# Which operand tiles of three Strassen stages start at a shifted SBUF address

## The chip, the cores and the metric

The kernel runs on one core of one Trainium2 chip. The metric is the device time of one execution in microseconds (us); lower is better. Before the change it is 2397.99 us, the median of three runs (2395.8 to 2398.48).

## The reference

One layer of a hybrid decoder over 16 meta tokens and 512 real tokens, width 2048, all in float32:

```python
u = rmsnorm(h, norm1_g[l])
proj = u @ w_in[l]                       # 2048 -> 10240
v_pool, v_lru, v_gelu, g_pool, g_lru = jnp.split(proj, IN_SPLITS, axis=-1)
pool_out = pool_mixer(v_pool, pool_w[l], pool_scale[l])
xc = causal_depthwise_conv(v_lru, conv_w[l], conv_b[l])
lru_out = rg_lru(xc, ...) * jax.nn.gelu(v_gelu)
merged = jax.nn.sigmoid(g_pool) * pool_out + jax.nn.sigmoid(g_lru) * lru_out
h = h + merged @ w_out[l]
u2 = rmsnorm(h, norm2_g[l])
h = h + jnp.square(jax.nn.relu(u2 @ mlp_w1[l])) @ mlp_w2[l]   # 2048 -> 8192 -> 2048
...
return rmsnorm(h, final_g)[:, N_META:]
```

## The kernel before

Every product is made from float32 split in two parts, `hi` (rounded) and `lo` (the rest), and three matmuls: weight hi by data hi, weight hi by data lo, weight lo by data hi. The helper `mm3` (its matmul is L365 of the profile) issues these three for one tile of 128 rows; the weights are the stationary operand, the data (128 x 256) the moving one. So the moving operand's start addresses follow the pattern hi, lo, hi for each tile.

The program has these stages, in this order: input projections with the recurrence and the pooling (PSUM tiles `ps_v`, `ps_vl`, `ps_vp`, `ga`, `ps_pw`), the *gates* (`ps_Agl`, `ps_Bge`, ... one pass of `strassen` for each of three segments and eight channel blocks, 24 passes), the output projection (`ps_wo`, 512 columns, no Strassen), *MLP 1* (`ps_A`, `ps_B`, `ps_C`, 32 passes), *MLP 2* (`ps_Ab`, `ps_Bb`, `ps_Cb`: two passes of `strassen_pair`, which take two t at a time, 27 of `strassen` for t = 5 to 31, then three pairs and a single one), and the last norm (`ps_w2l`, `ps_n`).

One pass of `strassen` is seven products in the order x11 (into A), t1 (B), t2 (A), x21 (C), t3 (A), x22 (B), t4 (A). In the gates and MLP 1 each product has eight tiles of data, that is 24 matmuls, and a pass has 168. The data of these seven operands stay in SBUF for the whole stage, in two large tiles `a1` and `a2`, at addresses that `place` gives and `fill` loads. Weights stream in through SP's queue (L104), and ACT (L134) and DVE (L135, L125) split and add them.

In MLP 2 the data are the *slots*: slot j is made by pass j of MLP 1, is stored to DRAM and loaded again into one of nine places (`places`, place j % 9) by POOL's queue (`load_slot`, L1023), 896 KB at a time, and is split into hi and lo by ACT (L1035) and DVE (L1036) in `split_slot`. Pass t (t = 8 to 31) uses the eight slots t-8 to t-1, one tile of each in every product; slot t is split in the middle of pass t and slot t+1 is loaded behind it.

Almost all data tiles start at the same address modulo 256 bytes. A few don't:

- gates: the eight tiles of x22 lie 264 elements apart and not 256, so tile k starts 32 k bytes further on, modulo 256;
- MLP 1: the same for t2;
- MLP 2: in six of the nine places the hi part of x11 alone is moved by 64 or 160 bytes (`gaps`, in elements); the lo part, and all other operands, are not.

What is set by address and what by order: PE's instructions stand in the order in which the program issues them; a scheduler places the work of the other engines, and each DMA queue is served in order.

Of the kernel before, what the change touches and what calls it, by code (L numbers as in the profile page):

```python
# [11 lines left out]
F32 = mybir.dt.float32  # L12
F32R = mybir.dt.float32r
# [4 lines left out]
P = 128  # L18
# [4 lines left out]
TH = T // 2  # L23
HS = SEQ // 2
# [7 lines left out]
B0 = META + HS  # L32
JS = 31
WIN = 8

ORDER = [(JS + q) % 8 for q in range(8)]

# [128 lines left out]
def build(ctx, tc, nc, xt_d, par_d, w_in_d, gate_d, pool_d, woa_d, wob_d, woc_d, w1_d, w2_d, w2t_d,  # L166
          out_d):
    V, S, G, PE = nc.vector, nc.scalar, nc.gpsimd, nc.tensor
# [31 lines left out]
    PL = 16 * TH  # L200
    a1_pool = ctx.enter_context(tc.tile_pool(name="a1", bufs=1))
    a1 = a1_pool.tile([P, 4 * PL + 6 * HS], F32R, name="a1")
# [1 line left out]
    ht = x_stage.enter_context(tc.tile_pool(name="xp", bufs=1)).tile([P, KD, T], F32, name="ht")  # L204
    a2 = None

    def place(i, width=HS):

        if width > HS:
            return [tuple(a1[:, i * PL + (8 * j + k) * width : i * PL + (8 * j + k) * width + HS]  # L210
                          for j in range(2)) for k in range(8)]
        if i < 6:
            t, at = (a1, i * PL) if i < 4 else (a2, (i - 4) * 16 * HS)
            return [tuple(t[:, at + (8 * j + k) * HS : at + (8 * j + k + 1) * HS] for j in range(2))
                    for k in range(8)]
        u = [a1[:, 4 * PL + u * HS : 4 * PL + (u + 1) * HS] for u in range(6)]
        u += [a2[:, 32 * HS + u * HS : 32 * HS + (u + 1) * HS] for u in range(10)]
        return [(u[k], u[8 + k]) for k in range(8)]

    def fill(i, src, n, width=HS):  # L220

        if width > HS:
            t = a1[:, i * PL : i * PL + 16 * width].rearrange("p (a k n) -> p a k n", a=2, k=8)
            src = src.rearrange("p a (k n) -> p a k n", k=8)
            for j in range(2):
                G.dma_start(t[:, j, n, :HS], src[:, j, n].bitcast(F32R))
        elif i < 6:
            t, at = (a1, i * PL) if i < 4 else (a2, (i - 4) * 16 * HS)
            n = slice(n.start * HS, n.stop * HS)
            t = t[:, at : at + 16 * HS].rearrange("p (a n) -> p a n", a=2)[:, :, n]  # L230
            G.dma_start(t, src[:, :, n].bitcast(F32R))
        else:
            flat = src.rearrange("p a n -> p (a n)").bitcast(F32R)
            G.dma_start(a1[:, 4 * PL :], flat[:, : 6 * HS])
            G.dma_start(a2[:, 32 * HS :], flat[:, 6 * HS :])
# [60 lines left out]
    def slots_of(t):  # L296
        return range(max(0, t - WIN), min(t, JS))

    for g in groups:
        def part(n, h):  # L300
            xs = [w2_d[t % WIN + 8 * n, h, :, slots_of(t)[0] * P : (slots_of(t)[-1] + 1) * P] for t in g]
            return xs if len(xs) > 1 else xs[0]
# [45 lines left out]
    y_sp = [dram.tile([P, (7 if j < JS else 4) * HS], F32, name=f"ysp{j}") for j in range(32)]  # L348
# [3 lines left out]
    f_sp = {r: dram.tile([P, 2, 8 * HS], F32, name=f"fsp_{r}") for r in ("x11", "t2", "x21", "t3", "x22", "t4")}  # L352
    g_sp = {r: dram.tile([P, 2, 8 * HS], F32, name=f"gsp_{r}") for r in ("t2", "t3", "x22", "t4")}
# [14 lines left out]
    with ExitStack() as mx:  # L368
# [68 lines left out]
        xc, xs, pend = {}, {}, []  # L437
# [184 lines left out]
        for kind, i in jobs:  # L622
            table[kind](i)
            if (kind, i) == ("VP", 15):
                for q, r in ((0, "x11"), (1, "t2"), (2, "x21"), (6, "t3")):
                    fill(q, f_sp[r], slice(0, 8))
                fill(3, f_sp["x22"], slice(0, 8), TH)
            elif (kind, i) == ("GA", 7):
                W.free["w21"] = 2
        fill(5, f_sp["t4"], slice(0, 8))  # L630
# [136 lines left out]
    def put_plain(e, by_half=False):  # L767
# [12 lines left out]

    X = {r: place(i, TH if r == "x22" else HS) for r, i in (
        ("x11", 0), ("t2", 1), ("x21", 2), ("x22", 3), ("t1", 4), ("t4", 5), ("t3", 6))}
    with tc.tile_pool(name="gp", bufs=1, side="right", reuse_waits="tile") as gp:
        for c in range(8):
# [30 lines left out]
    for i in range(8):  # L817
        G.dma_start(merged(i), m_sp[i].bitcast(F32R).rearrange("p (a s) -> p a s", a=4))

    X = {r: place(i, TH if r == "t2" else HS) for r, i in (  # L820
        ("t2", 0), ("t3", 1), ("x22", 2), ("t4", 3), ("x11", 4), ("t1", 5), ("x21", 6))}
    wo_stage = ExitStack()
    wo = wo_stage.enter_context(tc.tile_pool(name="wo", bufs=1, side="right", reuse_waits="tile"))
# [49 lines left out]
    def forms(p, h, u):  # L873
# [5 lines left out]
        t1, t2 = t[:, :HS], t[:, HS:]  # L879
        put_hl(x11, *X["x11"][p])  # L880
        put_hl(x21, *X["x21"][p])
# [24 lines left out]
    for ch in range(KD):  # L906
        hi, lo = W.next()
# [10 lines left out]
    def refill(q):  # L918

        r = ("t2", "t3", "x22", "t4")[q]  # L920
        fill(q, g_sp[r], slice(0, 6), TH if q == 0 else HS)
        if r in held:
            for i, x in enumerate(X[r][6]):
                G.dma_start(x, held[r][:, i * HS : (i + 1) * HS])
# [15 lines left out]
    for p in range(3, 6):  # L940
        h = None if p == 3 else load_x(p)
        ts3 = []
        for a in range(2):
            t = bank("wo", f"{p}_{a}", SEQ)
# [3 lines left out]
            if (p, a) == (3, 0):  # L948
# [4 lines left out]
                h = load_x(3)  # L953
# [5 lines left out]
    for i in range(2):  # L959
# [4 lines left out]
        for q in (2 * i, 2 * i + 1):  # L964
            hi, lo = W.next()
# [38 lines left out]
    def at(r, n=1):  # L1004
        i = SLOT.index(r)
        return slice(i * HS, (i + n) * HS)

    def shift(pool, name, n=8):

        V.memset(pool.tile([P, n], F32, name=name), 0.0)  # L1010

    slots, early, n = {}, late.enter_context(ExitStack()), 14 * HS
    gaps = {1: 16, 2: 40, 3: 16, 7: 40, 8: 16, 0: 40}
    places = {i: a[:, q * step : q * step + n + gaps.get(i, 0)]
              for a, held, step in ((a1, (1, 2, 3, 7, 8), n + 64), (a2, (4, 5, 6), n)) for q, i in enumerate(held)}

    def load_slot(j, queue):  # L1020
        if j < JS:
            s = slots[j] = places[j % (WIN + 1)]
            queue.dma_start(s[:, : 7 * HS].bitcast(F32), y_sp[j])  # L1023

    def slot(j, r):

        s, a = slots[j], slice(0, 6 * HS) if r is None else at(r)
        h = 13 * HS + gaps.get(j % (WIN + 1), 0) if r == "x11" else 7 * HS + a.start
        return s[:, h : h + a.stop - a.start], s[:, a]

    def split_slot(j):
# [12 lines left out]
    for j in range(32):  # L1044
        if j:
            y = yp.tile([P, 4 * HS], F32, tag="y", name=f"y{j}")
        if j == 1:
            s0 = early.enter_context(tc.tile_pool(name="s0", bufs=1, side="right", reuse_waits="tile"))
            places[0] = s0.tile([P, 14 * HS + 40], F32R, name="slot0")
            shift(s0, "shift0", 32)  # L1050

        def of(r, n=1):
            c = at(r, n)
            return y[:, c.start - 4 * HS : c.stop - 4 * HS]

        def put(c, x, z):
            o = of("x" + c)
            if z is not None:
                V.tensor_tensor(o, x, z, op=ALU.add)
            if c == "12":  # L1060
                o = of("x11", 2)
                V.scalar_tensor_tensor(o, o, 0.0, rho, op0=ALU.max, op1=ALU.mult)
            elif c[0] == "2":
                n = int(c[1]) - 1
                V.scalar_tensor_tensor(o, o if n else x, 0.0, rho[:, n * HS : (n + 1) * HS],
                                       op0=ALU.min, op1=ALU.mult)

        if j == 4:
            load_slot(0, nc.gpsimd)
        strassen(j, X.get, put, **{0: dict(head=head, middle=middle), 8: dict(between=lambda: split_slot(0)), 31: dict(hooks=last)}.get(j, {}))  # L1070
        S.activation(y, y, AF.Square)
        if j >= JS:
            if j < 31:
                nc.gpsimd.dma_start(y_sp[j], y)
            continue
        nc.gpsimd.dma_start(y_sp[j][:, 4 * HS :], y[:, : 3 * HS])
        x21, x22, x11, x12 = (of(r) for r in ("x21", "x22", "x11", "x12"))
        tt = yp.tile([P, 4 * HS], F32, tag="t", name=f"t{j}")
        t1, t2, t3, t4 = (tt[:, at(r)] for r in ("t1", "t2", "t3", "t4"))
        V.tensor_tensor(t1, x11, x12, op=ALU.subtract)  # L1080
        V.tensor_tensor(t3, x22, x12, op=ALU.subtract)
        V.scalar_tensor_tensor(t2, x22, -1.0, t1, op0=ALU.mult, op1=ALU.subtract)
        V.scalar_tensor_tensor(t4, t2, -1.0, x21, op0=ALU.mult, op1=ALU.subtract)
        nc.gpsimd.dma_start(y_sp[j][:, : 4 * HS], tt)
# [11 lines left out]
    for n, g in enumerate(groups):  # L1096
        t = g[0]
# [7 lines left out]
        if t < JS + 2:  # L1105
            for x, e in zip(g, es):
                nc.gpsimd.dma_start(h_sp[x % WIN], e, accum_op=ALU.add)
        if n < 4:
            load_slot(n + 5, nc.gpsimd)
        elif t >= WIN:  # L1110
            load_slot(t + 1, nc.gpsimd)
# [29 lines left out]
    n = 64 - 2 * JS  # L1141
# [35 lines left out]
    for i in range(2):  # L1177
        sums, alone = [], []
        for m in range(KD):
            if i == 0 and m % 4 == 0:  # L1180
                parts.append(W.next())
            hi, lo = parts[m // 4]
            t = ps.tile([P, 512], F32, tag="ps", name=f"ps_w2l_{i}_{m}")[:, :HS]
            c = slice(i * HS, (i + 1) * HS)
            for k in range(n):
                s = slice((m % 4) * n * P + k * P, (m % 4) * n * P + (k + 1) * P)
# [3 lines left out]
            h = ht[:, m // 2, i, m % 2]  # L1190
            V.tensor_tensor(h, t, h, op=ALU.add)  # L1191
            whole = m < 2
            q = hp.tile([P, HS], F32, tag=f"ss{m}" if whole else "ft", name=f"sqo{i}_{m}", bufs=2 if whole else 6)
# [11 lines left out]
            if i == 1 and m == 5:  # L1205
                r = root(0, pend)
# [5 lines left out]
    r = root(1, total(1, pend))  # L1212
# [50 lines left out]
```

## Time and profile before

| what | value |
|---|---|
| median of three runs | 2397.99 us |
| time of the profiled execution | 2397.97 us |
| its span, first to last instruction | 2396.2 us |
| PE busy | 2355.8 us (98%), 19254 matmuls |
| DVE, ACT, POOL busy | 1921.9 (80%), 1212.7 (51%), 313.1 us (13%) |
| TensorE clock granted, mean | 0.995 |

The profiled execution lies 0.02 us from the median, and 1.8 us of it is outside the span. PE is busy nearly all the time, but a busy PE is not yet a PE at its peak: records of matmuls overlap, and how far apart their starts lie says what one costs.

### The profile page before, as it was taken

To read this page: it belongs to the slowest core of one execution; us is meant where nothing else is said; L and a number is where in the kernel's file an instruction comes from. 1 tells how busy PE (TensorE), PEld (TensorE's weight loads), DVE (VectorE), ACT (ScalarE), POOL (GpSimd) and SP (SyncE) were. 2 spreads that over 40 slices of the span, in tenths; PEclk is the share of its full clock that TensorE was granted. 3 is DMA by queue.
4 is the path that set the end of the run, shared out by engine and by line. 5 is a ranking of instruction groups with operands and counts; after the bars stand their busy time and mean duration, and the time that the engine had idled before them with its cause. 6 is when DMAs were issued, how large, how long until landed. Compare 5 with 4: busy or idle time off the path is not lost. (4 is left out here: it accounts for less than half of the span.)

```text
span 2396.2 us, 46247 instructions
## 1 busy us (share of the span) xinstructions
PE 2355.8 (98%) x19254; PEld 2307.7 (96%) x19254; DVE 1921.9 (80%) x2357; ACT 1212.7 (51%) x1632; POOL 313.1 (13%) x429
## 2 busy tenths in 40 slices
PE   8999999999999999999999999999989999999997
PEld 8999999999999999887999999999989999999997
DVE  7867766588888887378989888888879888888877
ACT  6654645355555554244444444444455555555545
POOL 0224342300000001033000000000010000000013
PEclk9999999999999999999999999999999999999999
DMA  5255555754444447568544444555576666666663
GB/s 198 89 167 170 174 176 165 255 190 147 142 149 142 149 152 260 181 202 285 179 161 152 156 157 154 164 165 162 168 226 173 182 178 184 192 187 182 180 184 111
DMA packets 118354, 418.73 MB, mean 175 GB/s; under 512 B 14016, under 2 KB 21312, under 8 KB 116480
## 3 DMA queue, kind: packets, MB, share of 16 engines
q1 hardware_dynamic: 77040, 253.40, 33.0%
q0 software_dynamic: 40960, 162.29, 21.1%
q8 instruction: 150, 2.46, 0.4%
q14 instruction: 60, 0.49, 0.1%
q10 hardware_dynamic: 144, 0.10, 0.0%
HBM read 324.89 MB, written 90.31 MB: 173 GB/s over the span
## 5 line engine op out<-in xcount | busy, mean ns | idle before, releaser
L135 DVE TENSOR_TENSOR wlo<-raw,whi 128x1024 fp32r<-128x1024 f32 (+2 forms) x388 | 466.7, 1205 | 123.5 <-ACT whi L134 122.6
L134 ACT ACTIVATE whi<-raw 128x1024 fp32r<-128x1024 f32 (+2 forms) x388 | 399.0, 1034 | 323.3 <-issue 81.4
L134 ACT ACTIVATE whi<-sum 128x1024 fp32r<-128x1024 f32 (+3 forms) x267 | 278.8, 1044 | 451.1 <-DVE sum L125 229.2
L135 DVE TENSOR_TENSOR wlo<-sum,whi 128x1024 fp32r<-128x1024 f32 (+3 forms) x267 | 320.1, 1199 | 73.5 <-ACT whi L134 67.7
L365 PE MATMUL ps_A<-a,whi 128*128 128x256 f32 x2048 | 358.0, 278 | 0.0
L365 PE MATMUL ps_Ab<-a,whi 128*128 128x256 f32 x1728 | 309.0, 279 | 3.7 <-DVE a L1036 1.8
L365 PEld LDWEIGHTS ps_A<-a,whi 128*128 128x128 f32 x2048 | 310.3, 188 | 1.1 <-issue 1.0
L365 PE MATMUL ps_A<-a,wlo 128*128 128x256 f32 x1024 | 284.0, 277 | 0.0
L365 PEld LDWEIGHTS ps_Ab<-a,whi 128*128 128x128 f32 x1728 | 263.2, 189 | 4.4 <-DVE a L1036 2.0
L365 PE MATMUL ps_Ab<-a,wlo 128*128 128x256 f32 x864 | 240.4, 278 | 0.0
L125 DVE TENSOR_TENSOR sum<-sum,raw 128x1024 f32<-128x1024 f32 (+4 forms) x178 | 213.8, 1201 | 5.5
L365 PEld LDWEIGHTS ps_A<-a,wlo 128*128 128x128 f32 x1024 | 192.8, 188 | 0.0
L365 PE MATMUL ps_B<-a,whi 128*128 128x256 f32 x1024 | 177.5, 276 | 0.0
L365 PEld LDWEIGHTS ps_Ab<-a,wlo 128*128 128x128 f32 x864 | 163.4, 189 | 0.0
L365 PE MATMUL ps_vl<-a,whi 128*128 128x272 f32 (+1 forms) x896 | 163.3, 285 | 0.0
L365 PE MATMUL ps_vp<-a,whi 128*128 128x256 f32 (+1 forms) x896 | 162.8, 284 | 0.0
L365 PE MATMUL ps_wo<-a,whi 128*128 128x512 f32 x512 | 158.0, 390 | 0.0
L365 PEld LDWEIGHTS ps_B<-a,whi 128*128 128x128 f32 x1024 | 154.2, 188 | 0.0
L365 PE MATMUL ps_Bb<-a,whi 128*128 128x256 f32 x864 | 153.5, 278 | 0.0
L365 PE MATMUL ps_B<-a,wlo 128*128 128x256 f32 x512 | 141.4, 276 | 0.0
L365 PEld LDWEIGHTS ps_vl<-a,whi 128*128 128x128 f32 x896 | 138.2, 189 | 0.3
L365 PEld LDWEIGHTS ps_vp<-a,whi 128*128 128x128 f32 x896 | 138.2, 188 | 0.0
(334 smaller groups left out, 5827.5 us busy)
## 6 DMA issues: line engine op xcount, KB each, us to landing
raw<-w SPq DMA_DIRECT2D x168, 512.0 KB, 4.2
raw<-w_in SPq DMA_DIRECT2D x135, 512.0 KB, 3.7
w<-w SPq DMA_DIRECT2D x56, 512.0 KB, 4.2
a<-ysp POOLq DMA_DIRECT2D x27, 896.0 KB, 6.3
hsp<-e POOLq DMA_DIRECT2D x33, 512.0 KB, 5.9
ysp<-t POOLq DMA_DIRECT2D x31, 512.0 KB, 4.9
w<-w_in SPq DMA_DIRECT2D x24, 512.0 KB, 3.7
ysp<-y POOLq DMA_DIRECT2D x31, 384.0 KB, 5.0
```

The costliest lines, as they stand in the source:

```text
L125: nc.vector.tensor_tensor(self.raw[o], self.raw[x], self.raw[y], op=ALU.add)
L134: nc.scalar.activation(hi[:, s], raw[:, s], AF.Copy)
L135: nc.vector.tensor_tensor(lo[:, s], raw[:, s], hi[:, s].bitcast(F32), op=ALU.subtract)
L365: PE.matmul(o, a, b, start=first and i == 0, stop=last and i == 2, skip_group_check=True)
```

## The change

Fewer tiles are shifted, and where one is, hi and lo are shifted by the same amount. In the gates only the eighth tile of x22 is (by 56 elements, 224 bytes). In MLP 1 the seventh tile of t2 is shifted by 8 elements (32 bytes) and the eighth by 56 (224 bytes). In MLP 2, in two of nine places (2 and 7), x11's hi and lo are shifted by 56 elements; all the rest is unshifted modulo 256 bytes. The number of matmuls whose moving operand is shifted goes from 504 to 72 in the gates, from 672 to 192 in MLP 1, from 352 to 168 in MLP 2.

The loads follow. x22 is filled by one DMA of seven tiles and one of the eighth where there were two (one for hi, one for lo) of 1 KB pieces. t2's refill is one DMA and not two. A slot of an odd place is loaded by two DMAs (six operands and x11) and not one. A memset that padded the place of slot 0 falls away.

```diff
+ODD = 56
+ODD_GATES, ODD_MLP = {7: ODD}, {6: 8, 7: ODD}
...
-    def place(i, width=HS):
-        if width > HS:
-            return [tuple(a1[:, i * PL + (8 * j + k) * width : i * PL + (8 * j + k) * width + HS]
-                          for j in range(2)) for k in range(8)]
+    def place(i, odd=None):
+        if odd:
+            at = [[i * PL + j * 8 * TH + k * HS + odd.get(k, 0) for j in range(2)] for k in range(8)]
+            return [tuple(a1[:, x : x + HS] for x in xs) for xs in at]
...
-    def fill(i, src, n, width=HS):
-        if width > HS:
-            ...
-            for j in range(2):
-                G.dma_start(t[:, j, n, :HS], src[:, j, n].bitcast(F32R))
+    def fill(i, src, n, odd=None):
+        if odd:
+            t = a1[:, i * PL : i * PL + 16 * TH].rearrange("p (a n) -> p a n", a=2)
+            cut = min(n.stop, *odd)
+            G.dma_start(t[:, :, : cut * HS], src[:, :, : cut * HS].bitcast(F32R))
+            for k in range(cut, n.stop):
+                at = k * HS + odd.get(k, 0)
+                G.dma_start(t[:, :, at : at + HS], src[:, :, k * HS : (k + 1) * HS].bitcast(F32R))
...
-    X = {r: place(i, TH if r == "x22" else HS) for r, i in (
+    X = {r: place(i, ODD_GATES if r == "x22" else None) for r, i in (
...
-    X = {r: place(i, TH if r == "t2" else HS) for r, i in (
+    X = {r: place(i, ODD_MLP if r == "t2" else None) for r, i in (
...
-    gaps = {1: 16, 2: 40, 3: 16, 7: 40, 8: 16, 0: 40}
-    places = {i: a[:, q * step : q * step + n + gaps.get(i, 0)]
+    odd_places = (2, 7)
+    places = {i: a[:, q * step : q * step + n + (64 if i in odd_places else 0)]
...
-            queue.dma_start(s[:, : 7 * HS].bitcast(F32), y_sp[j])
+            if j % (WIN + 1) in odd_places:
+                queue.dma_start(s[:, : 6 * HS].bitcast(F32), y_sp[j][:, : 6 * HS])
+                queue.dma_start(s[:, 6 * HS + ODD : 7 * HS + ODD].bitcast(F32), y_sp[j][:, 6 * HS :])
+            else:
+                queue.dma_start(s[:, : 7 * HS].bitcast(F32), y_sp[j])
...
-        h = 13 * HS + gaps.get(j % (WIN + 1), 0) if r == "x11" else 7 * HS + a.start
+        if r == "x11":
+            lo = 6 * HS + (ODD if odd else 0)
+            return s[:, lo + HS : lo + 2 * HS], s[:, lo : lo + HS]
+        a = slice(0, 6 * HS) if r is None else at(r)
+        h = 8 * HS + (64 if odd else 0) + a.start
...
-            places[0] = s0.tile([P, 14 * HS + 40], F32R, name="slot0")
-            shift(s0, "shift0", 32)
+            places[0] = s0.tile([P, 14 * HS + 8], F32R, name="slot0")
```

In the gates and in MLP 1, PE's instructions stand in the same order in both programs; only addresses differ. On POOL's queue, in the middle of MLP 2, the loads of the slots (`ysp` is the DRAM copy of a slot, `a_84` the tile `a1`, `hsp` the running sum in DRAM) stand like this before; slot 11 is `ysp_134`:

```order
L1107 DMA hsp_115<-e_20795 128x1024
L1023 DMA a_84<-ysp_133 128x1792
L1107 DMA hsp_116<-e_21024 128x1024
L1023 DMA a_84<-ysp_134 128x1792
L1107 DMA hsp_117<-e_21253 128x1024
L1023 DMA a_84<-ysp_135 128x1792
```

and like this after:

```order
L1115 DMA hsp_115<-e_20794 128x1024
L1028 DMA a_84<-ysp_133 128x1792
L1026 DMA a_84<-ysp_134 128x256
L1115 DMA hsp_116<-e_21023 128x1024
L1025 DMA a_84<-ysp_134 128x1536
L1115 DMA hsp_117<-e_21252 128x1024
L1028 DMA a_84<-ysp_135 128x1792
```

Of the slot in an odd place (11 % 9 = 2), the small x11 part now stands one place ahead, before the accumulation of the pass's result; the large part stands where the whole load stood.

Ahead of the gates, POOL's queue fills x22 (`fsp_x_183`) before in this way, between the last pooling work:

```order
L231 DMA a_84<-fsp_x_181 128x4096
L559 TENSOR_TENSOR pw_2_5329<-pw_1_5327 128x525
L234 DMA a_84<-fsp_t_182 128x1536
L559 TENSOR_TENSOR pw_4_5331<-pw_2_5329 128x521
L226 DMA a_84<-fsp_x_183 128x8x256
L559 TENSOR_TENSOR pw_8_5333<-pw_4_5331 128x513
L226 DMA a_84<-fsp_x_183 128x8x256
```

and after in this:

```order
L236 DMA a_84<-fsp_x_181 128x4096
L564 TENSOR_TENSOR pw_2_5329<-pw_1_5327 128x525
L239 DMA a_84<-fsp_t_182 128x1536
L564 TENSOR_TENSOR pw_4_5331<-pw_2_5329 128x521
L228 DMA a_84<-fsp_x_183 128x2x1792
L564 TENSOR_TENSOR pw_8_5333<-pw_4_5331 128x513
L231 DMA a_84<-fsp_x_183 128x2x256
```

The two fills keep their places; what differs is the size and the pieces of each. At the start of MLP 2, where two passes share their weights, about ten rows of PE's order trade places among themselves; nothing is added there.

More of the change, by code (lines that the diff above doesn't have):

```diff
@@ L218, in place @@
         return [(u[k], u[8 + k]) for k in range(8)]
-    def fill(i, src, n, width=HS):
-        if width > HS:
-            t = a1[:, i * PL : i * PL + 16 * width].rearrange("p (a k n) -> p a k n", a=2, k=8)
-            src = src.rearrange("p a (k n) -> p a k n", k=8)
-            for j in range(2):
-                G.dma_start(t[:, j, n, :HS], src[:, j, n].bitcast(F32R))
+    def fill(i, src, n, odd=None):
[6 more added lines that the diff above has]
+                G.dma_start(t[:, :, at : at + HS], src[:, :, k * HS : (k + 1) * HS].bitcast(F32R))
         elif i < 6:
@@ L626, in build @@
                     fill(q, f_sp[r], slice(0, 8))
-                fill(3, f_sp["x22"], slice(0, 8), TH)
+                fill(3, f_sp["x22"], slice(0, 8), ODD_GATES)
             elif (kind, i) == ("GA", 7):
@@ L920, in refill @@
         r = ("t2", "t3", "x22", "t4")[q]
-        fill(q, g_sp[r], slice(0, 6), TH if q == 0 else HS)
+        fill(q, g_sp[r], slice(0, 6), ODD_MLP if q == 0 else None)
         if r in held:
@@ L1006, in at @@
         return slice(i * HS, (i + n) * HS)
-    def shift(pool, name, n=8):
-        V.memset(pool.tile([P, n], F32, name=name), 0.0)
     slots, early, n = {}, late.enter_context(ExitStack()), 14 * HS
-    gaps = {1: 16, 2: 40, 3: 16, 7: 40, 8: 16, 0: 40}
-    places = {i: a[:, q * step : q * step + n + gaps.get(i, 0)]
+    odd_places = (2, 7)
+    places = {i: a[:, q * step : q * step + n + (64 if i in odd_places else 0)]
               for a, held, step in ((a1, (1, 2, 3, 7, 8), n + 64), (a2, (4, 5, 6), n)) for q, i in enumerate(held)}
@@ L1022, in load_slot @@
             s = slots[j] = places[j % (WIN + 1)]
-            queue.dma_start(s[:, : 7 * HS].bitcast(F32), y_sp[j])
-    def slot(j, r):
-        s, a = slots[j], slice(0, 6 * HS) if r is None else at(r)
-        h = 13 * HS + gaps.get(j % (WIN + 1), 0) if r == "x11" else 7 * HS + a.start
+            if j % (WIN + 1) in odd_places:
[3 more added lines that the diff above has]
+                queue.dma_start(s[:, : 7 * HS].bitcast(F32), y_sp[j])
+    def slot(j, r):
+        s, odd = slots[j], j % (WIN + 1) in odd_places
+        if r == "x11":
[3 more added lines that the diff above has]
+        h = 8 * HS + (64 if odd else 0) + a.start
         return s[:, h : h + a.stop - a.start], s[:, a]
```

## The prediction

> **What bounds the kernel now.** I read the page's head first, then busy time by stage, then the starts of PE's matmuls in the timeline, and last the chain of work that ended last.
>
> ```profile
> span 2396.2 us, 46247 instructions
> PE 2355.8 (98%) x19254; PEld 2307.7 (96%) x19254; DVE 1921.9 (80%) x2357; ACT 1212.7 (51%) x1632; POOL 313.1 (13%) x429
> ```
>
> The stretches below are the gates, MLP 1, the start of MLP 2 and its long even part (columns: from and to, length, then busy time and count of PE, PEld, DVE, ACT, POOL, then the granted clock, the DMA share, GB/s).
>
> ```profile
> 479.05:947.15 468.10, 463.39 (x4033) 462.50 (x4032) 402.57 (x400) 248.66 (x310) 20.40 (x38) 1.00 0.47 161
> 1122.20:1741.70 619.50, 616.15 (x5380) 614.92 (x5379) 551.38 (x693) 299.25 (x364) 41.43 (x76) 1.00 0.52 167
> 1741.70:1820.00 78.30, 69.95 (x547) 66.96 (x546) 65.99 (x86) 45.87 (x76) 6.22 (x8) 0.96 0.69 199
> 1820.00:2316.00 496.00, 496.00 (x4334) 496.00 (x4333) 412.51 (x414) 256.78 (x334) 38.15 (x55) 1.00 0.63 181
> ```
>
> PE never idles from 1820 to 2316 us, at full clock, and DVE, the next, is busy 83%. So PE's spacing of starts is the time. One pass through the seven products is 168 matmuls at most. In the timeline a tile gives a row "whi x2" (weight hi by data hi and lo) and a row "wlo x1"; the distance between two "whi x2" rows is three matmuls. This is the segment gp of channel block 1 in the gates: product t3, then x22, then t4.
>
> ```profile
> 593.84 0.39 PE L365 MATMUL ps_Agp<-a,whi 128*128 128x256 f32 x2
> ...
> 596.56 0.39 PE L365 MATMUL ps_Bgp<-a,whi 128*128 128x256 f32 x2
> 596.90 0.40 PE L365 MATMUL ps_Bgp<-a,whi 128*128 128x256 f32 x2
> 597.25 0.40 PE L365 MATMUL ps_Bgp<-a,whi 128*128 128x256 f32 x2
> ...
> 599.39 0.40 PE L365 MATMUL ps_Agp<-a,whi 128*128 128x256 f32 x2
> 599.74 0.39 PE L365 MATMUL ps_Agp<-a,whi 128*128 128x256 f32 x2
> 600.08 0.39 PE L365 MATMUL ps_Agp<-a,whi 128*128 128x256 f32 x2
> ```
>
> The unshifted product takes 596.56 - 593.84 = 2.72 us for eight tiles: 0.34 a tile, 113 ns a matmul. x22, same shapes, has its first tile unshifted (0.34) and then 0.35 to 0.36 a tile. Its eight tiles and the two of t4 behind it take 600.08 - 596.56 = 3.52 us where ten tiles at 0.34 take 3.40. So the seven shifted tiles cost 0.12 us. MLP 1 pays the same for t2 (the first tiles of t2 and of x21 behind it: 1156.68 - 1153.16 = 3.52):
>
> ```profile
> 1153.16 0.39 PE L365 MATMUL ps_A<-a,whi 128*128 128x256 f32 x2
> ...
> 1155.99 0.40 PE L365 MATMUL ps_C<-a,whi 128*128 128x256 f32 x2
> 1156.34 0.39 PE L365 MATMUL ps_C<-a,whi 128*128 128x256 f32 x2
> 1156.68 0.39 PE L365 MATMUL ps_C<-a,whi 128*128 128x256 f32 x2
> ```
>
> But a shift does something else too. Unshifted products don't always go at 2.72. Segment ge of block 0, from its x11 on, then its x22 and t4:
>
> ```profile
> 505.77 0.40 PE L365 MATMUL ps_Age<-a,whi 128*128 128x256 f32 x2
> ...
> 508.60 0.40 PE L365 MATMUL ps_Bge<-a,whi 128*128 128x256 f32 x2
> ...
> 519.90 0.40 PE L365 MATMUL ps_Bge<-a,whi 128*128 128x256 f32 x2
> ...
> 522.75 0.40 PE L365 MATMUL ps_Age<-a,whi 128*128 128x256 f32 x2
> 523.10 0.39 PE L365 MATMUL ps_Age<-a,whi 128*128 128x256 f32 x2
> 523.44 0.39 PE L365 MATMUL ps_Age<-a,whi 128*128 128x256 f32 x2
> ```
>
> Here x11 takes 2.83 us, and the pass keeps that pitch up to x22 (five products in 519.90 - 505.77 = 14.13); behind x22's shifted tiles the pitch is 0.34 again. So PE has two steady modes at the same addresses, 113 and 118 ns a matmul. It stays in one until something disturbs it, a stall or a shifted tile. The chain shows the same in MLP 2 (start, length, what): t = 12, and t = 13 behind it.
>
> ```profile
> 1898.95 5.51 PE ps_Ab L365 x48
> 1904.46 2.83 PE ps_Bb L365 x24
> 1907.29 2.83 PE ps_Ab L365 x24
> ...
> 1918.60 5.66 PE ps_Ab L365 x48
> 1924.26 2.74 PE ps_Bb L365 x24
> 1927.00 2.72 PE ps_Ab L365 x24
> ...
> 1937.88 5.55 PE ps_Ab L365 x48
> ...
> 2077.45 2.83 PE ps_Bb L365 x24
> ...
> 2250.42 2.83 PE ps_Bb L365 x24
> ```
>
> After the shifted tiles of its x11 (second half of the first row), t = 12 goes at 2.83; x11 of t = 13 brings it back. A pass at 2.83 costs 7 x 0.11 = 0.77 us more. The last two rows are in t = 21 and t = 30: three passes at 2.83, nine apart as the places are. An ordinary pass pays for x11 alone: 5.55 - 2 x 2.72 = 0.11, and 0.01 to 0.02 in the row behind it, 0.12 in all.
>
> **The price of one shifted tile** of the new kind (224 bytes, hi and lo alike, between unshifted tiles) stands nowhere. The nearest row is the first tile of x11 at t = 11, whose hi alone is shifted, with unshifted tiles on both sides:
>
> ```profile
> 1882.02 0.39 PE L365 MATMUL ps_Ab<-slot,whi 128*128 128x256 f32 x2
> ...
> 1882.36 0.40 PE L365 MATMUL ps_Ab<-a,whi 128*128 128x256 f32 x2
> ...
> 1882.71 0.40 PE L365 MATMUL ps_Ab<-a,whi 128*128 128x256 f32 x2
> ...
> 1883.07 0.39 PE L365 MATMUL ps_Ab<-a,whi 128*128 128x256 f32 x2
> ```
>
> It and the unshifted tile behind take 1883.07 - 1882.36 = 0.71 where two take 0.68: 0.03 us. The lower end is a seventh of x22's 0.12, 0.017; the upper is 0.05, since each start is printed to 0.01. I take 0.03, an isolated tile like those to come. For MLP 1's pair of adjacent tiles I take 0.045, between two sevenths of 0.12 (0.034) and two isolated ones (0.06).
>
> **The change part by part.** PE is the bound in all three stages, so a saving there is the time's, as far as the supply holds.
>
> - Gates: 24 passes x (0.12 - 0.03) = 2.2 us.
> - MLP 1: 32 x (0.12 - 0.045) = 2.4 us.
> - MLP 2: at t = 8 to 31 a pass has 16/9 odd slots on the mean, 0.055 us. 21 ordinary passes: 21 x (0.12 - 0.055) = 1.4. The three passes at 2.83, if they don't come again: 3 x (0.77 - 0.055) = 2.1. The passes with fewer slots at both ends have fewer shifted tiles; I count nothing for them (upper bound 14 passes x 0.07 = 1).
> - Passes that a stall leaves at 2.83 at a stage's head (gates: the rows of ge above): counted as they are; if the one tile brings PE back a pass sooner 0.8 less, a pass later 0.8 more.
> - Loads of the odd slots: seven more DMAs on POOL. The row of a plain load, the split that needs it, and the issues:
>
> ```profile
> 1995.84 0.56 POOL L1023 DMA_DIRECT2D a<-ysp  x1 [14.47 <-PE ps_Ab L365]
> ...
> 2007.50 1.78 ACT L1035 ACTIVATE a<-a 128x1536 fp32r<-128x1536 f32 x2
> ...
> a<-ysp POOLq DMA_DIRECT2D x27, 896.0 KB, 6.3
> ```
>
> The split comes 11.7 us after the issue and the load lands in 6.3, so 5.4 us cover a second issue of 0.56. POOL waited 14.5 us before it, and the second, small DMA stands even earlier in the queue. I count zero; were that cover gone, 7 x 0.56 = 3.9 us. What is queued behind it on POOL is the accumulation into `hsp`; the tile that it reads is written again two passes later.
> - x22's and t2's fills (one DMA fewer, pieces up to 7 KB): no wait of PE in the trace is on them; zero. The memset: zero, one DVE instruction among 2357.
> - Supply: DVE, at 402.57 of 468.10 us in the gates and 551.38 of 619.50 in MLP 1, has more room than the 0.5% that PE gains.
>
> Sum: 2.2 + 2.4 + 1.4 + 2.1 = 8.1 us, from the execution's own 2397.97: **2389.9**, which against the median 2397.99 is the same. With the price of a tile at its ends (24 single, 32 pairs, 43 in MLP 2) the sum moves by -1.8 to +1.2; with the head passes and the spread of the runs before (2.7 us) the likeliest case reaches from 2387 to 2393.
>
> **The rivals.**
>
> *The 118 ns mode stays (slower).* One tile is less of a kick than seven. From 113 ns it may end in 118, as five shifted tiles do at t = 12; from 118 it may not come back, and a stage that starts there then stays there. Against it: nearly every block of shifted tiles in the trace, long or short, ends at 113 ns, the single one at t = 11 among them. For it: those at t = 12 that don't, and nothing shows a 224-byte step with hi and lo alike. The map from address pattern to mode is the same in each pass, so a stage fails whole: 24 x 0.77 = 18.5 us in the gates or in MLP 2, 24.6 in MLP 1. That is 2408 for one stage, 2430 for two. It decides from 8.1/0.77 = 11 passes of 80 at 2.83, and is slower by 0.2% from 17.
>
> *The 118 ns mode in some passes (about the same).* As now at t = 12, a few positions in the cycle of nine, or every second pass of one stage: 6 to 15 passes at 2.83, 4.6 to 11.6 us: 2394 to 2401.
>
> *The addresses don't matter (same).* If a matmul's pitch hung on its shape alone, nothing would change: 2398. The rows of x22 against t3 speak against it, 0.35 to 0.36 and 0.34. The Trainium skill says it: "TensorE: Matmul & The Clock Gate", section "Back-to-back issue gap", has N / 2.4 + 2.5 ns, 109.2 for 256 columns, whatever the address; its "Step-by-step: what each phase is for" says that PE has two independent read ports, so loading the next weights takes no bandwidth from a running matmul. By that rule the sum is zero. The trace, with 113 and 118 ns for one shape, agrees with neither the figure nor the independence of the address.
>
> *The second load is late:* 3.9 us less gained, 2394.
>
> **How the numbers follow.** A comparison of this kernel can tell about 0.2%, 4.8 us, from no change. The forecast gets 0.62; whole stages 0.17; some passes 0.12; no effect 0.05; late loads 0.04. Faster by over 0.2% (under 2393.2): 0.62 + 0.04 of those with some passes + 0.02 of the late loads = 0.68. Slower (over 2402.8): 0.17 + 0.01 = 0.18. Within: 0.14. The range runs from 2386.5, the forecast's lower end with the head passes sooner back, to 2405, past the cases of some passes, and leaves the whole stages at 118 ns and a little at the bottom outside.
>
> **What would show it.** Right: x22 and t2 rows at 2.75 to 2.77 us; t = 12, 21, 30 at 2.72 a product; PE busy without a break from 1820 on. Wrong: unshifted products at 2.83 in long stretches of any stage (the 118 ns mode), or a wait of PE or of ACT L1035 on the odd slots' DMAs (late loads), or x22 still 0.12 over (price mis-sized). A stall that moves at the start of MLP 2, where order trades places and PE idles 78.30 - 69.95 = 8.35 us at a clock of 0.96, would add or take one or two us that no term holds.

## The result and the profile after

The changed kernel takes 2387.87 us, the median of five runs (2386.67 to 2391.19), against 2398.48 for five runs of the kernel before (2395.80 to 2401.08): ratio 0.9964, 95% interval 0.9953 to 0.9975. Timed once more later, beside other kernels, it was 2386.82 against 2395.56: 0.9963, 0.9950 to 0.9975. Its profiled execution took 2389.73 us, 8.2 less than that of before. The head of its page:

```profile
span 2388.0 us, 46263 instructions
PE 2347.3 (98%) x19254; PEld 2300.1 (96%) x19254; DVE 1922.5 (81%) x2356; ACT 1212.3 (51%) x1632; POOL 315.5 (13%) x435
```

The number of matmuls is the same, PE is as busy, and all the other engines do the same work. PE's work takes less time, so I look at its pace. Busy time over three stretches of 420 us in which PE never stops, one in each stage (gates, MLP 1, MLP 2), first before:

```profile
500.00:920.00 420.00, 420.00 (x3679) 420.00 (x3678) 366.12 (x359) 224.45 (x279) 15.53 (x29) 1.00 0.44 147
1180.00:1600.00 420.00, 420.00 (x3685) 420.00 (x3684) 374.77 (x464) 203.66 (x244) 23.74 (x44) 1.00 0.49 158
1850.00:2270.00 420.00, 420.00 (x3670) 420.00 (x3670) 352.97 (x352) 220.41 (x284) 30.48 (x43) 1.00 0.63 183
```

and after:

```profile
500.00:920.00 420.00, 420.00 (x3702) 420.00 (x3701) 366.87 (x360) 225.59 (x280) 15.52 (x29) 1.00 0.44 148
1180.00:1600.00 420.00, 420.00 (x3701) 420.00 (x3701) 376.02 (x465) 204.57 (x245) 23.71 (x44) 1.00 0.50 159
1850.00:2270.00 420.00, 420.00 (x3701) 420.00 (x3700) 353.95 (x353) 220.84 (x285) 33.38 (x48) 1.00 0.64 185
```

The fourth column holds the count of matmuls. At 113.33 ns each, 420 us hold 3706; before it was 21 to 36 short of that, now it is 4 or 5. PE is 100% busy in all six rows: the count shows the gain, the busy share can't.

From the timeline, the x22 that the prediction showed (gates, segment gp, block 1): where x22 starts, where t4 starts, and t4's third tile. Then the same for t2 and x21 in MLP 1:

```profile
595.62 0.39 PE L370 MATMUL ps_Bgp<-a,whi 128*128 128x256 f32 x2
...
598.35 0.40 PE L370 MATMUL ps_Agp<-a,whi 128*128 128x256 f32 x2
...
599.04 0.39 PE L370 MATMUL ps_Agp<-a,whi 128*128 128x256 f32 x2
```

```profile
1148.00 0.39 PE L370 MATMUL ps_A<-a,whi 128*128 128x256 f32 x2
...
1150.75 0.40 PE L370 MATMUL ps_C<-a,whi 128*128 128x256 f32 x2
...
1151.43 0.39 PE L370 MATMUL ps_C<-a,whi 128*128 128x256 f32 x2
```

x22 and two tiles take 3.42 us and not 3.52, t2 and two tiles 3.43: 0.02 and 0.03 over the 3.40 of ten unshifted tiles. In MLP 2, t = 12, 16, 21 and 30 in the chain of waits:

```profile
1893.10 5.47 PE ps_Ab L370 x48
1898.57 2.73 PE ps_Bb L370 x24
...
1969.41 5.46 PE ps_Ab L370 x48
...
2070.25 2.73 PE ps_Bb L370 x24
...
2241.93 2.73 PE ps_Bb L370 x24
```

The three passes at 2.83 are gone; 2.73 is the tail of an odd tile that ends x11. A pass with one odd slot pays 0.02 (5.46), one with two 0.04.

The whole account, from the starts of all matmuls in the two traces. "Pace" adds up what a start lies beyond 113.33 ns behind the one ahead of it, for distances up to 131 ns; "stalls" does so for longer ones, which takes in matmuls at half the granted clock.

| part | length before, after | pace before, after | stalls before, after |
|---|---|---|---|
| up to the gates | 479.05, 477.46 | | |
| gates | 467.21, 466.46 | 3.81, 0.92 | 7.35, 9.49 |
| output projection | 175.91, 175.91 | | |
| MLP 1 | 619.51, 614.26 | 4.13, 1.42 | 5.87, 3.33 |
| MLP 2 | 614.41, 614.33 | 6.22, 1.86 | 17.95, 22.22 |
| behind it | 40.08, 39.54 | | |

Pace gains 9.96 us; stalls take back 3.9 and the parts that the change doesn't touch give 2.1. So MLP 2 has the largest gain in pace, 4.4 us, and is as long as before in this pair of executions.

### The profile page after: what moved, and what is told of

Same layout as the page of the kernel before. It is cut to its first block, busy times and chain, and to the rows that moved or that the text cites. A ratio compares the mean times of both kernels' runs of the same rounds, so it can differ in the third digit from the quotient of the medians.

```text
span 2388.0 us, 46263 instructions
## 1 busy us (share of the span) xinstructions
PE 2347.3 (98%) x19254; PEld 2300.1 (96%) x19254; DVE 1922.5 (81%) x2356; ACT 1212.3 (51%) x1632; POOL 315.5 (13%) x435
## 5 line engine op out<-in xcount | busy, mean ns | idle before, releaser
L128 DVE TENSOR_TENSOR sum<-w,raw 128x1024 f32<-128x1024 f32 (+3 forms) x89 | 106.5, 1197 | 40.1 <-DMA raw<-w 39.7
```

Of the source, the lines that this page charges most:

```text
L128: nc.vector.tensor_tensor(self.raw[o], self.raw[x], self.raw[y], op=ALU.add)
```

## The experiments

**No shifted tile at all.**

```diff
-ODD = 56
+ODD = 0
-ODD_GATES, ODD_MLP = {7: ODD}, {6: 8, 7: ODD}
+ODD_GATES, ODD_MLP = {7: ODD}, {6: 0, 7: ODD}
```

> The changed kernel with every shift set to zero (ODD = 0, and 0 for the seventh tile of t2): the same DMAs and the same order, but no moving operand of the three stages is shifted. Theory (two steady modes, the one odd tile is what brings PE back to 113 ns): each stage meets a stall near its start, falls to 118 ns there and nothing brings it back, so up to 24 x 0.77 = 18.5 us more in the gates, 24.6 in MLP 1, 18.5 in MLP 2: 2410 to 2450 us, with unshifted products at 2.83 us in stretches of many passes. Rival (a shifted tile is only a cost, and fewer of them is all of the gain): 24 x 0.03 + 32 x 0.045 + 24 x 0.055 = 3.5 us less than the changed kernel, 2384 us, all products at 2.72.

Seven runs lie anywhere from 2384.13 to 2425.90 us: 2384.1, 2389.4, 2401.0, 2419.2, 2420.7, 2425.6, 2425.9. One of them was profiled, the slowest (2425.90); the same kind of stretches in it:

```profile
500.00:920.00 420.00, 420.00 (x3569) 420.00 (x3568) 355.89 (x349) 217.86 (x269) 14.99 (x29) 1.00 0.42 143
1180.00:1600.00 420.00, 420.00 (x3567) 419.87 (x3567) 364.19 (x452) 197.79 (x237) 23.20 (x43) 1.00 0.48 153
1850.00:2270.00 420.00, 420.00 (x3708) 420.00 (x3707) 357.19 (x357) 222.75 (x288) 33.34 (x48) 1.00 0.64 186
```

The gates and MLP 1 stand at 117.7 ns a matmul (420 us / 3569), at full clock; MLP 2, in the same execution and as unshifted as they are, at 113.3. By the starts, 3910 matmuls of the gates follow each other in the 118 ns mode, and 4991 of MLP 1: until the stage ends. In MLP 1 it begins here (starts of tiles, timeline):

```profile
1182.89 0.39 PE L370 MATMUL ps_B<-a,whi 128*128 128x256 f32 x2
...
1183.33 0.50 PE L370 MATMUL ps_A<-a,whi 128*128 128x256 f32 x2
...
1183.79 0.40 PE L370 MATMUL ps_A<-a,whi 128*128 128x256 f32 x2
...
1184.14 0.40 PE L370 MATMUL ps_A<-a,whi 128*128 128x256 f32 x2
```

Two distances of 0.44 and 0.46 where 0.34 stood, and behind them 0.35: two starts in a row, each 0.1 us late, are enough. The theory holds in the main: two modes, a break can change one for the other, and where neither a break nor a shifted tile comes, PE stays as it is. A break can also bring it back: MLP 1 of this execution began at 118, and a break of 3.1 us in its first pass left it at 113. In the same way MLP 2, which the theory had at 118 too, came out of the breaks at its start at 113. The rival fits the best run, 2384.13, which is no better than the best of the changed kernel (2383.68), and perhaps the one of 2389.39; the other five lie above every run of the changed kernel (up to 2392.56) and show what the odd tile pays for. Only the slowest has a trace; that the others differ by the stages they spend at 118 ns is read from their times.

**The three parts alone.** Gates in the code of before; MLP 1 likewise; MLP 2 in the changed kernel with the two others put back. For instance

```diff
-                fill(3, f_sp["x22"], slice(0, 8), TH)
+                fill(3, f_sp["x22"], slice(0, 8), ODD_GATES)
...
-    X = {r: place(i, TH if r == "x22" else HS) for r, i in (
+    X = {r: place(i, ODD_GATES if r == "x22" else HS) for r, i in (
```

> The kernel before with the gates part of the change alone (x22: one tile shifted and not seven). Theory: x22 loses 24 x (0.12 - 0.03) = 2.2 us by the prediction's prices, 2.9 by the spacing of the starts in the trace of the changed kernel; so 2.2 to 2.9 us less than before, 2395.5 us against a median of 2398.5, and the gates' stretch shorter by that, give or take 2 us for stalls at its head. Rival (gain from elsewhere, the addresses of x22 don't matter): 2398.5.

> The kernel before with the MLP 1 part alone (t2: two tiles shifted and not seven). Theory: 32 x (0.12 - 0.045) = 2.4 us by the prediction's prices, 2.7 by the spacing of the starts in the changed kernel's trace: 2395.8 us against 2398.5, MLP 1 shorter by 2.4 to 2.7 plus or minus 2.5 for the stall near its start. Rival (the stall at the start of MLP 1, 2.5 us shorter in the changed kernel, belongs to the change): 5 us less, 2393.5.

> The changed kernel with gates and MLP 1 as before: the MLP 2 part alone (two odd places of nine, hi and lo alike). Theory: 3.5 us by the prediction's terms (1.4 + 2.1), 4.4 by the spacing of the starts in the changed kernel's trace, if the stalls at the start of MLP 2 are those of before; 2394 to 2395 us. Rival (the 4.3 us of longer stalls and half-clock stretches at the start of MLP 2 in the changed kernel's profile belong to the new layout and loads): the gain is eaten, 2398 to 2399, with PE's idle time at 1741 to 1820 us larger by 4 than before.

| part | median (10 runs each) | before (28 runs) | ratio, 95% interval | pace of its stage in its trace |
|---|---|---|---|---|
| gates | 2392.65 | 2397.34 | 0.9979 (0.9970 to 0.9988) | 1.15 |
| MLP 1 | 2395.21 | 2397.34 | 0.9987 (0.9977 to 0.9996) | 1.33 |
| MLP 2 | 2393.26 | 2397.34 | 0.9984 (0.9974 to 0.9994) | 1.95 |

Each part gains, and none of the intervals reaches 1. The medians give 4.7 + 2.1 + 4.1 = 10.9 us, the pace alone 2.7 + 2.8 + 4.3 = 9.8. The gates' median is 2 us more than the pace explains; its interval, 2.9 to 7.2 us, holds both. The rival for MLP 1, 5 us because its shorter stall belongs to the change, is not borne out: the part gives 2.1.

These traces also show how much a stage varies by itself. The kernel before, and the parts that leave a stage as it was, pay 3.0 to 3.8 us of pace in the gates, 4.1 to 5.4 in MLP 1 and 6.0 to 8.0 in MLP 2 (three traces each). With the changed layout it is 0.6 to 1.5, 1.3 to 1.9 and 1.6 to 2.0 in all traces here that have it. The ranges stay apart, though a single pair of traces gives each gain to no better than a microsecond or two. The spread comes from the heads and ends of the stages: for t = 8 to 31 of MLP 2 each pass pays the same in all three executions of the old layout, 0.715 us at t = 12, 21 and 30 every time. In that even stretch the addresses decide the mode, and not chance.

The rival for MLP 2 was that its longer stalls belong to the new layout. At its start PE waited for ACT's `u_b` (the waits of PE: us in total, times, longest), here before, after, and with the MLP 2 part alone:

```profile
PE ps_Ab L365 <- ACT u_b L741: 1.7, 1, 1.7
```

```profile
PE ps_Ab L370 <- ACT u_b L746: 3.3, 1, 3.3
```

```profile
PE ps_Ab L368 <- ACT u_b L744: 2.2, 1, 2.2
```

and the busy time of that stretch, after and then with the part alone:

```profile
1734.20:1812.50 78.30, 68.52 (x529) 65.83 (x528) 64.03 (x85) 44.36 (x75) 6.79 (x9) 0.93 0.69 197
```

```profile
1736.00:1815.00 79.00, 68.69 (x559) 65.17 (x559) 64.27 (x85) 45.95 (x76) 7.41 (x11) 1.00 0.71 212
```

With the same layout the wait is 2.2 us, the granted clock there is 1.00 and not 0.93, and MLP 2 is 609.76 us long, 4.7 less than before, nearly all of it pace (6.22 before, 1.95 here). So the stalls of the profiled execution of after are not a fixed price of the layout. Whether a little of them is stays open: all stalls of MLP 2 are 17.9, 18.0 and 19.8 us in the three traces with the old layout, 17.6 to 22.8 in the eleven with the new one.

**One shifted tile in MLP 1.**

```diff
-ODD_GATES, ODD_MLP = {7: ODD}, {6: 8, 7: ODD}
+ODD_GATES, ODD_MLP = {7: ODD}, {7: ODD}
```

> The changed kernel with one shifted tile of t2 in MLP 1 (the eighth, by 224 bytes) where it has two; the seventh is unshifted. Theory (one tile is enough to bring PE back, each costs its own price): every pass behind the first t2 at 2.72 us a product; the price of t2's shifted tiles falls from about 0.03 us a pass to about 0.015 to 0.02, so MLP 1 is 0.3 to 0.5 us shorter at the same stalls, which the time alone can't show. Rival (the step of 32 bytes ahead of it is needed): unshifted products at 2.83 us over many passes of MLP 1, up to 24 us more, 2390 to 2412.

2384.36 us in its single run. The eighth tile of t2, the first of x21 and the third of x21:

```profile
1148.00 0.40 PE L370 MATMUL ps_A<-a,whi 128*128 128x256 f32 x2
1148.35 0.40 PE L370 MATMUL ps_C<-a,whi 128*128 128x256 f32 x2
...
1149.04 0.39 PE L370 MATMUL ps_C<-a,whi 128*128 128x256 f32 x2
```

Three tiles, one of them shifted, in 1.04 us where three take 1.02. Summed over single starts, which are known to the ns, a shifted tile costs 20.0 ns on the mean, the pair of the changed kernel 33.3, seven of before 120.0. No pass of MLP 1 stays at 2.83, but that alone doesn't show that one tile is enough: PE came out of the first pass, in which it waits, at 113 ns, and no later shifted tile of MLP 1 was reached at 118. The gates of this trace, with their one tile, do show it: two x22 were reached at 118, and PE left both at 113. For MLP 1 the kernel with the fewest tiles below has two such places: behind the first PE stayed at 118, behind the second it was at 113. Leaving out the second tile is worth 0.4 us, less than the time can tell.

**Hi alone.**

```diff
-            at = [[i * PL + j * 8 * TH + k * HS + odd.get(k, 0) for j in range(2)] for k in range(8)]
+            at = [[i * PL + j * 8 * TH + k * HS + (odd.get(k, 0) if j == 0 else 0) for j in range(2)] for k in range(8)]
```

and the same for the slots and the fills.

> The changed kernel with the same places shifted in hi alone; lo stays at the unshifted address (one DMA more for each shifted tile of x22 and t2). Theory A (what brings PE back is a step of the address, and a hi, lo, hi pattern that goes there and back makes two of them): it comes back too, a shifted tile costs about twice as much, 0.03 us as the single hi-only tile at t = 11 before; 2389 us. Theory B (only a step taken by all three matmuls of a tile resets PE; with hi alone it may end in either mode, as at t = 12 before): stretches of whole passes at 2.83 us, 0.77 each, in at least one stage: 2395 to 2430.

2388.62 us (four runs; 0.9958, 0.9943 to 0.9974). Theory B's stretches don't come: no shifted tile takes PE from 113 to 118. Theory A is right with a limit: of three tiles of this kind that PE reached in the 118 ns mode one brought it back and two did not (one of them was followed by another that did). The kind of the changed kernel has the limit too: in the gates and MLP 1 of all traces here with 224 bytes in hi and lo, 13 places were reached at 118 (without the first t2 of MLP 1, inside which PE waits); behind 10 of them PE was at 113, behind 3 only one pass later. x22's eight tiles and t4's first two, from the first row to the last:

```profile
597.28 0.39 PE L371 MATMUL ps_Bgp<-a,whi 128*128 128x256 f32 x2
...
600.71 0.39 PE L371 MATMUL ps_Agp<-a,whi 128*128 128x256 f32 x2
```

3.43 us where hi and lo alike have 3.42; by the starts 33.3 ns a tile against 20.0: dearer, though not the double.

**Every slot in two DMAs.**

```diff
-            if j % (WIN + 1) in odd_places:
+            if True:
+                o = ODD if j % (WIN + 1) in odd_places else 0
```

> The changed kernel with every slot of MLP 2 loaded by two DMAs, not only those of the two odd places: 20 more DMAs on POOL, addresses unchanged. Theory (the load is covered by 5.4 us before the split that needs it): no difference, 2388 us, PE without a break from 1820 us on. Rival (a second load is late or holds up the accumulation behind it): up to 20 x 0.56 = 11 us more, 2390 to 2399, with a wait of ACT's split or of PE on a DMA.

2388.39 us (0.9967, 0.9953 to 0.9981), as the changed kernel. The loads of the slots after, then here (KB each, median us from issue to landing), and, last, busy time from 1820 us on, after and then here:

```profile
a<-ysp POOLq DMA_DIRECT2D x20, 896.0 KB, 6.1
...
a<-ysp POOLq DMA_DIRECT2D x7, 128.0 KB, 4.1
```

```profile
a<-ysp POOLq DMA_DIRECT2D x27, 768.0 KB, 5.7
...
a<-ysp POOLq DMA_DIRECT2D x27, 128.0 KB, 3.8
```

```profile
1820.00:2300.00 480.00, 480.00 (x4229) 480.00 (x4228) 403.36 (x403) 253.41 (x330) 39.92 (x57) 1.00 0.63 183
```

```profile
1820.00:2300.00 480.00, 480.00 (x4229) 480.00 (x4228) 403.69 (x404) 253.09 (x330) 49.38 (x74) 1.00 0.64 182
```

With 20 more DMAs PE has no break, and 4229 matmuls in that stretch are as many as in the changed kernel. The cover is enough for a second load of every slot.

**A shifted tile in the input projections.**

```diff
-        return a1[:, at : at + B0], a1[:, at + XW - HS : at + XW]
+        b = at + XW - HS - (8 if k == KD - 1 else 0)
+        return a1[:, at : at + B0], a1[:, b : b + HS]
```

> The changed kernel with one shifted tile more, in the input projections: of the sixteen tiles of 256 columns the last (k = 15) starts 32 bytes earlier, hi and lo alike; nothing else is moved. In the changed kernel's trace the 1728 matmuls of 256 columns there start 118 ns apart, not 113, and the 1728 of 272 columns 124 ns, where 113.3 x 272 / 256 = 120.4. Theory (the whole stage stands in the 118 ns mode because nothing in it is shifted): one tile of sixteen brings it to 113 and 120.4, 1728 x 4.3 + 1728 x 3.5 = 13.5 us less the price of 108 x 2 shifted triples at 0.02 (4 us at most): 2374 to 2379 us. Rival (the change from 272 to 256 columns after every few matmuls, not a mode, makes the pitch): no difference or a little more, 2388 to 2392.

A miss: 2389.31 us (0.9962, 0.9949 to 0.9975). Busy time of the projections after, then here:

```profile
20.00:460.00 440.00, 438.73 (x3484) 431.42 (x3484) 304.51 (x455) 229.10 (x326) 131.93 (x143) 1.00 0.48 158
```

```profile
20.00:460.00 440.00, 438.64 (x3484) 431.19 (x3483) 302.77 (x455) 229.48 (x326) 131.69 (x143) 1.00 0.48 158
```

3484 matmuls in both. Where 272 and 256 columns take turns, 124 and 118 ns are the pitch, and a tile shifted by 32 bytes takes nothing off. It doesn't show what makes that pitch. Nor does it rule out the theory: 32 bytes is the one distance that, in the three stages below, never brought PE back, and other distances weren't tried here.

**The distance of the shift**, 128 and 32 bytes for 224, with one tile in MLP 1:

```diff
-ODD = 56
+ODD = 32      # and 8 in the second kernel
-ODD_GATES, ODD_MLP = {7: ODD}, {6: 8, 7: ODD}
+ODD_GATES, ODD_MLP = {7: ODD}, {7: ODD}
```

> The changed kernel with one shifted tile in each of the three stages (in MLP 1 the eighth alone, as in e5_one), and the shift is 128 bytes where it is 224 (ODD = 32). Theory (what PE feels is the start address modulo 128 bytes; in the trace of before the fifth tile of x22, shifted by 128, goes like an unshifted one): nothing is shifted by that measure, so it goes as e1_zero does: a stage that a stall leaves in the 118 ns mode stays there, runs from 2384 to 2426 us, and the eighth tile costs nothing. Rival (any step of the address resets PE): 2384 to 2390 us, as e5_one.

With 128 bytes five runs take 2385.46, 2387.13, 2391.61, 2404.91 and 2425.78 us, spread out as with no shift. The profiled one (2387.13) was at 113 ns nearly throughout, but one place tells: the last x22 of the gates, reached in the 118 ns mode. Its first tile, t4's first and t4's eighth with 128 bytes, then with 224 (the kernel with one shifted tile in MLP 1):

```profile
938.37 0.40 PE L370 MATMUL ps_Bgp<-a,whi 128*128 128x256 f32 x2
...
941.20 0.40 PE L370 MATMUL ps_Agp<-a,whi 128*128 128x256 f32 x2
...
943.67 0.40 PE L370 MATMUL ps_Agp<-a,whi 128*128 128x256 f32 x2
```

```profile
938.43 0.40 PE L370 MATMUL ps_Bgp<-a,whi 128*128 128x256 f32 x2
...
941.26 0.39 PE L370 MATMUL ps_Agp<-a,whi 128*128 128x256 f32 x2
...
943.64 0.39 PE L370 MATMUL ps_Agp<-a,whi 128*128 128x256 f32 x2
```

Both x22 take 2.83. Then seven tiles take 2.47 us (0.353 each) behind 128 bytes and 2.38 (0.340) behind 224. Here a step of 128 bytes did not bring PE back. One place would not show more, since 3 of 13 places with 224 bytes did not either; the runs of 2404.91 and 2425.78 us, which have no trace, speak for it as well, since every pass of the gates and MLP 1 has such a tile. So half of the theory is likely and not shown. The other half is wrong: the tile isn't free, by the starts it costs the same 20 ns. Its ground was wrong too: in the trace of before the fifth tile of x22 takes 0.358 us, as its neighbours do (0.357 to 0.359), and not 0.340.

> As e5_one, with a shift of 32 bytes where it is 224 (ODD = 8). Theory (any step that is not a multiple of 128 bytes brings PE back at the same price): 20 ns for a shifted tile, all passes behind the first one at 2.72 us a product, 2384 to 2390 us. Rival (the distance counts): stretches at 2.83 us, 0.77 us for each pass, or another price for the tile, 33 ns or more.

With 32 bytes it is 2441.88 us (two runs, 2440.25 and 2443.52; 1.0189, 1.0171 to 1.0208), the slowest kernel here. The stretches again:

```profile
500.00:920.00 420.00, 420.00 (x3568) 420.00 (x3568) 356.27 (x349) 217.85 (x269) 15.36 (x29) 1.00 0.42 143
1180.00:1600.00 420.00, 420.00 (x3568) 420.00 (x3567) 363.29 (x451) 197.01 (x237) 23.19 (x43) 1.00 0.47 153
1850.00:2270.00 420.00, 420.00 (x3567) 420.00 (x3567) 347.42 (x344) 213.56 (x275) 31.95 (x46) 1.00 0.62 178
```

In these stretches all three stages stand in the 118 ns mode throughout. The rival holds, and more strongly than I had put it: this step doesn't only fail to bring PE back, in the trace it takes it from 113 to 118 once in the gates and five times in MLP 2 (three at its start, two at its end), and never the other way. In MLP 1 a break in the first pass put PE at 118, and the shifted tiles of the 31 passes behind it left it there. So the distance decides which way a tile can take PE.

**The fewest tiles, and the changed kernel again.**

```diff
-ODD_GATES, ODD_MLP = {7: ODD}, {6: 8, 7: ODD}
+ODD_GATES, ODD_MLP = {7: ODD}, {7: ODD}
...
-    odd_places = (2, 7)
+    odd_places = (2,)
```

> The fewest shifted tiles that still bring PE back in each stage: one tile of x22, one of t2, and in MLP 2 one odd place of nine (2) where the changed kernel has two. Theory: against the changed kernel 32 x (33.3 - 20.0) ns = 0.43 us less in MLP 1 and about 20 x 20 ns = 0.4 us less in MLP 2, 0.8 us in all: 2387.1 against 2387.9 us, which only the spacing of the starts can tell from no change. Rival (one pass in nine of MLP 2 has no odd slot then, and a stall ahead of it leaves passes at 2.83): 0.77 us more for each such pass, one to three of them, 2388 to 2390.

> The changed kernel itself, timed again beside the kernel before and e11_least on the same chip. Theory: the difference from before is the sum of the three parts measured alone (4.7 + 2.1 + 4.1 = 10.9 us): 2386 to 2388 against 2397.4. Rival (the parts help or hinder one another): off from that sum by over 3 us.

2389.07 us (2385.40 to 2390.43) and 2386.82 (2383.68 to 2392.56), each over five runs, against 2395.56: the times can't tell the two apart. The pace can (MLP 1 and MLP 2):

```profile
1180.00:1600.00 420.00, 420.00 (x3704) 420.00 (x3704) 376.37 (x466) 204.25 (x244) 23.72 (x44) 1.00 0.49 159
1850.00:2270.00 420.00, 420.00 (x3705) 420.00 (x3704) 354.35 (x354) 221.27 (x287) 32.27 (x46) 1.00 0.64 185
```

3704 and 3705 matmuls where the changed kernel has 3701 twice, 0.3 to 0.5 us in 420, as worked out; no whole pass of MLP 2 stays at 2.83. Over the whole of MLP 1 this trace pays more pace all the same, 2.3 us against 1.4 and 1.9 in the two traces of the changed kernel, because PE came out of the first pass at 118 and the shifted tile of the second left it there. It is the cheapest set tried, but a kernel that beats the changed one by more than the runs can show was not found. The changed kernel against before is 8.7 us here (6.0 to 12.0 by the interval) and the three parts alone gave 10.9: the parts add up, as far as can be told.

## Why the prediction was right

- **The bound.** Right: a saving in PE's pace came out as time, and PE is without a break from 1820 to 2300 us.
- **The mechanism.** Right: shifted tiles have a price, PE has two modes, and one tile of 224 bytes is enough of a kick, though not each time (10 of 13 places). That the address pattern settles the mode alike in each pass holds in the even part of MLP 2; behind a stall it doesn't.
- **The price of a tile** (taken at 0.03 us, range 0.017 to 0.05). Too high: 0.020. The row that I took it from, t = 11 before, has hi alone shifted, and that costs 0.033, as the hi-only kernel shows. For hi and lo alike the lower end was the better value. MLP 1's pair, taken at 0.045, costs 0.033. Seven tiles were right (0.120).
- **Gates**, forecast 2.2: 24 x (0.120 - 0.020) = 2.4, and 0.5 more at the head, where fewer matmuls stood in the 118 ns mode than before. This second part was in the forecast as "0.8 less or more".
- **MLP 1**, forecast 2.4: 32 x (0.120 - 0.033) = 2.8; the trace has 2.7.
- **MLP 2**, forecast 3.5: 4.4. The 21 ordinary passes gave 1.7 and not 1.4 (a pass now pays 0.02 to 0.04, taken as 0.055), the three at 2.83 gave 2.0 as forecast 2.1 (0.72 each before, 0.04 now), and the passes at both ends, which I had counted as nothing with an upper bound of 1, gave 0.7.
- **The sum.** Pace gained 10.0 where 8.1 was forecast. That the profiled execution moved by 8.2, to 2389.73 against the forecast 2389.9, is partly luck: stalls took 3.9 back and other stages gave 2.1. The medians, 10.6 and 8.7 less, are nearer to what pace alone says.
- **Loads, fills, memset at zero.** Right; 20 further DMAs cost nothing either.
- **Stalls that move** ("one or two us that no term holds"). The place was right, the size too small: in single stages they moved by -2.5 to +4.3. The gates' head and MLP 1's first wait, each before and then after:

```profile
PE ps_Bgl L365 <- ACT po L581: 0.4, 1, 0.4
...
PE ps_r L988 <- DVE ssq L854: 3.3, 1, 3.3
```

```profile
PE ps_Bgl L370 <- ACT po L586: 1.5, 1, 1.5
...
PE ps_r L993 <- DVE ssq L859: 1.8, 1, 1.8
```

  One is 1.1 longer, the other 1.5 shorter. All stalls of MLP 1 range from 2.7 to 5.9 us in the three traces with the old layout and from 2.1 to 4.3 with the changed one, so a difference of this size between two single traces says nothing about the change.
- **The rivals.** "The 118 ns mode stays" did not come, but its mechanism is real and was priced about right: with 32 bytes all three stages stand there nearly whole and the kernel is 55.1 us above the changed one on the same chip (2441.88 and 2386.82), where the prediction's stages add up to 18.5 + 24.6 + 18.5 = 61.6. With no shift it comes in one stage or another by chance. It hung on the number 224, and nothing in the profile of before could show that: on this point the forecast was lucky. "The addresses don't matter" is refuted by the same two kernels. The Trainium skill's figure for the gap of a single isolated matmul ("TensorE: Matmul & The Clock Gate", "Back-to-back issue gap", 109.2 ns for 256 columns) is met in no stage: the best stretch has 113.3, and 113.3 and 117.7 appear for the same instructions at the same addresses, at a granted clock of 1.00.

Open: why PE has the two modes, and which step leads to which. In t2 of the changed kernel a step of 32 bytes stands ahead of 224 and the pass ends at 113, so the last step seems to decide; that was not tried by itself.

## What to carry to other kernels

A PE that is 100% busy at full clock can still run 4% below its pace: count matmuls over a stretch without breaks, and compare the count with the best stretch of the same shape. Where a long stage of equal matmuls shows two paces, one tile at another address can bring the better one back for 20 ns, but the distance has to be tried on the chip, since 224 bytes restored it in 10 of 13 places, 128 did not in the one place seen, and 32 destroyed it. A layout whose runs scatter (2384 to 2426 here) is not better for its best run.

## What the hardware showed that I had not expected

- Two starts in a row, each 0.1 us late, were enough to put PE into the 118 ns mode for the 4991 matmuls to the end of the stage.
- The price of a shifted tile was the same for 128 and 224 bytes (20.0 ns, reached at 113 ns). What a tile leaves behind was not: mostly 113 ns for 224 bytes, 118 for 32, and for 128, in the one place seen, the mode as it was.
- With 272 and 256 columns in turn the pitch is 124 and 118 ns, with the one shift tried (32 bytes) as without; the 113 ns mode was seen only in stages of one width.
